# LayerNorm of the conv head: statistics spread through DRAM and applied in the channel layout, in place of a second set of transposes

## The chip, the cores and the metric

The kernel runs on one core of a Trainium2 chip. The metric is the device time of one execution in microseconds (us). Shown with the kernel before are three timed runs, and one further execution that the hardware profiler recorded instruction by instruction; durations and waits below are from that one. The engines are named as in the profile: PE (TensorE matmul) and PEld (its weight load), DVE (VectorE), ACT (ScalarE), POOL (GpSimd), SP (SyncE, whose queue issues every DMA of this kernel).

## The reference

One layer of a hybrid encoder in fp32 over two sequences (256 and 2048 tokens, with 16 meta tokens prepended). RMSNorm, one input projection of 1024 to 2816 columns, a windowed attention group, a convolution group, gates, one output projection, residual. The part around the change is the convolution group:

```python
def conformer_conv(c_val, c_glu, conv_w, conv_b, ln_w, ln_b):
    u = c_val * jax.nn.sigmoid(c_glu)
    y = depthwise_conv(u, conv_w, width=31) + conv_b        # over time, per channel
    return jax.nn.silu(layernorm(y, ln_w, ln_b))            # over the 512 channels of a token

cnv   = conformer_conv(...) * jax.nn.silu(g_conv)
mixed = jnp.concatenate([att, cnv], axis=-1)
out   = z + jnp.einsum('ble,ed->bld', mixed, w_out)
```

So each token needs a mean and a variance over its 512 channels, and is then scaled, shifted (per channel) and passed through SiLU.

## The kernel before

**Tiling.** Tokens go in 18 blocks of 128 (two of the prompt, sixteen of the sample) and six groups of three blocks. The input projection is cut into eleven units of 256 columns. It runs in two halves, c = 0 (groups 0 to 2) and c = 1 (groups 3 to 5); in each half the units come in the order: four conv units, two conv gates, two attention gates, one k/v unit, two q units. Every projection is a PSUM tile `pj` of 24 matmuls (eight pieces of the inner dimension, three passes each with the high and low parts of a split fp32), and projections are numbered pj1, pj2 and so on. Through most of the first stage a projection takes PSUM banks tagged "a" and "b" in turn, two of each, so projection n takes the bank of projection n-4.

**The q units.** A projection of a q unit (24 matmuls of 256 columns) is squared and summed on ACT (`ssq`), POOL makes the reciprocal root (`rqq`, lines 148 and 149), and DVE multiplies PSUM by it (`qs`, line 1010). Only then is the bank free. In c = 0 the second q unit is pj68 to pj76, block 0 to 8; pj77 is the first projection of c = 1, and from there a projection has 384 columns.

**The conv group.** The product u of value and gate lies with channels on partitions (four tiles of 128 channels, j = 0 to 3) and time along the free axis. The 31 taps of the convolution run on DVE into `y`, which again has channels on partitions.

**LayerNorm, one block at a time** (`ln_block`, line 211 on). Stage s1: four PE transposes (`lnt`, line 221) bring 128 tokens by 512 channels into a PSUM bank of tag "c", tokens on partitions. DVE takes bn_stats and bn_aggr, and POOL makes the reciprocal deviation r and -mean*r (`mv`, three small operations, lines 148, 149, 227). Stage s2: one DVE tensor_scalar from PSUM makes the normalised block `zn`, a scalar pair per partition (line 234). Stage s3: four PE transposes back (`lnu`, line 240), then four ACT SiLU (line 243) with the channels' weight and bias as per-partition scale and bias. Then `zn` is stored to a DRAM buffer `cd`. The blocks of c = 0 are done while the q units of c = 0 and the first conv units of c = 1 run; those of c = 1 during the q units of c = 1.

**What sets the order.** A clock of ticks runs through the program, about one per projection; `later(k, f)` puts a step k ticks on, and `owe` and a credit pace the conv taps among the projections. A scheduler then orders each engine's instructions at build time, by its own estimate of times; on the chip each engine runs its list in order and waits on semaphores. From the call of `attention_open` on (in the q units of c = 1), POOL keeps the program's order. In the second stage each block's attention and its output projection (`y`, line 609) alternate on PE. It reads the normalised conv blocks back from `cd` (`cn`), multiplies them on POOL by the gate `gc`, and splits the product into high and low parts (`mch`, `mcl`). The tiles `gc`, `cn`, `ga` and others of that stage take the memory of the LayerNorm tiles (`mixing_open` closes one pool and opens the other).

SP issues its DMAs in order, and each waits until the one eight before it has landed, since eight semaphores are used in turn.

Of the kernel before, what the change touches and what calls it, by code (L numbers as in the profile page):

```python
# [11 lines left out]
F32 = mybir.dt.float32  # L12
# [35 lines left out]
W0 = 3  # L48
LN_WAIT = (9, 1)
LTAGS = "dbdbd" + "dcdcddddd"  # L50
LTAGS_N = len(LTAGS)
# [48 lines left out]
def hymba_kernel(  # L100
# [24 lines left out]
    cd = dram.tile([NB, P, 512], F32, name="cd")  # L125
    wod = dram.tile([8, 2, P, D], F32, name="wod")

    ident = const.tile([P, P], F32, name="ident")
# [78 lines left out]
    cp = right_pools.enter_context(tc.tile_pool(name="cp", bufs=4, side="right"))  # L207
    yt = {}
    phase = [1]

    def ln_block(c, b, ready):
# [6 lines left out]
        def s1():  # L218
            pt = psum.tile([P, 512], F32, tag="c", name=f"lnt{b}")
            for j in range(NJ):  # L220
                nc.tensor.transpose(pt[:, P * j : P * j + P], yt[c, j][:, o : o + P], ident)
            bs = yp.tile([P, 6], F32, tag="bs", name=f"bs{b}")
            mv = yp.tile([P, 3], F32, tag="mv", name=f"mv{b}")
            nc.vector.bn_stats(out=bs, in_=pt)
            nc.vector.bn_aggr(out=mv[:, 0:2], in_=bs)
            rsqrt(mv[:, 1:2], mv[:, 1:2], 1.0, LN_EPS)
            nc.gpsimd.tensor_scalar(mv[:, 2:3], mv[:, 0:1], mv[:, 1:2], -1.0, op0=ALU.mult, op1=ALU.mult)
            st["pt"], st["mv"] = pt, mv
            later(1, s2)

        def s2():
            st["zn"] = yp.tile([P, 512], F32, tag="zn", name=f"zn{b}", bufs=3)
            mv = st["mv"]
            nc.vector.tensor_scalar(st["zn"], st["pt"], mv[:, 1:2], mv[:, 2:3], op0=ALU.mult, op1=ALU.add)
            later(1, s3)

        def s3():
            pt = psum.tile([P, 512], F32, tag="d" if phase[0] == 1 else "a", name=f"lnu{b}")
            for j in range(NJ):
                nc.tensor.transpose(pt[:, P * j : P * j + P], st["zn"][:, P * j : P * j + P], ident)  # L240
            cn = st["zn"].rearrange("p (j n) -> p j n", n=P)
            for j in range(NJ):
                nc.scalar.activation(
                    cn[:, j, :], pt[:, P * j : P * j + P], AF.Silu, bias=lb[:, j : j + 1], scale=lw[:, j : j + 1]
                )
            later(1, lambda: nc.sync.dma_start(cd[b], st["zn"]))

# [32 lines left out]
    def mixing_open():  # L280

        while ln_q:
            tick(0)
        flush(max(0, 4 - clock[0] + ln_at[0]))
        y_pools.close()
# [415 lines left out]
    if True:  # L701
        rows0 = {}
        sq0 = yp.tile([P, YW], F32, tag="y", name="sq0")

# [4 lines left out]
        def stats(i):  # L709
# [5 lines left out]
            elif i == 4:  # L715
                xn = yp.tile([P, YW], F32, tag="y", name=f"xn{i}")[:, :D]
            else:
# [90 lines left out]
        def weights(k):  # L808
# [4 lines left out]
            def load(eng):  # L813
# [8 lines left out]
                for q in range(4):  # L822
                    if k == 1:
                        if q % 2 == 0:
                            pair = yp.tile([P, YW], F32, tag="y", name=f"wraw{k}_{q}")
                        raw[q] = pair[:, 512 * (q % 2) : 512 * (q % 2) + 512].rearrange("p (a n) -> p a n", n=UW)
# [97 lines left out]
        def conv(c, j, part):  # L924
# [4 lines left out]
            def alloc():  # L929
                yt[c, j] = yp.tile([P, YW], F32, tag="y", name=f"y{c}_{j}")  # L930
                if c == 1:
                    nc.scalar.copy(yt[c, j][:, 0:YC], ycarry[:, j, :])

            def tap(k):
                y, u = yt[c, j], us[c, j]
                if k == 0:
# [86 lines left out]
        def kv_block(ws, g, o, rows, b):  # L1023
# [8 lines left out]
            kn = sp.tile([P, KV, 2, HD], F32, tag="kn", name=f"kn{b}")  # L1032
            owe(800)

# [285 lines left out]
```

## Time and profile before

| | |
|---|---|
| median of 3 runs | 948.61 us (948.51 to 950.12) |
| the profiled execution | 947.32 us |
| its span, first to last instruction | 945.3 us |
| granted TensorE clock | 1.000 |
| PE busy | 938.1 us (99% of the span) |
| DVE, ACT, POOL busy | 748.8, 424.1, 296.7 us |
| DMA moved | 176.49 MB, mean 187 GB/s |

A group row of the profile reads: line, engine, operation, output tile <- input tiles, shapes, count, then busy time and mean duration in ns of one, then the idle time of its engine just before it with what ended it. A row for a stretch gives each engine's busy time with its count of instructions in brackets. PE's matmuls overlap: a record of 270 ns can be followed by the next after 109 ns, so the cost of a matmul on PE is read from the distance of starts.

### The profile page before, as it was taken

To read this page: it belongs to the slowest core of one execution; us is meant where nothing else is said; L and a number is where in the kernel's file an instruction comes from. 1 tells how busy PE (TensorE), PEld (TensorE's weight loads), DVE (VectorE), ACT (ScalarE), POOL (GpSimd) and SP (SyncE) were. 2 spreads that over 40 slices of the span, in tenths; PEclk is the share of its full clock that TensorE was granted. 3 is DMA by queue.
4 is the path that set the end of the run, shared out by engine and by line. 5 is a ranking of instruction groups with operands and counts; after the bars stand their busy time and mean duration, and the time that the engine had idled before them with its cause. 6 is when DMAs were issued, how large, how long until landed. Compare 5 with 4: busy or idle time off the path is not lost.

```text
span 945.3 us, 16681 instructions
## 1 busy us (share of the span) xinstructions
PE 938.1 (99%) x5813; PEld 887.7 (94%) x5813; DVE 748.8 (79%) x1263; ACT 424.1 (45%) x1160; POOL 296.7 (31%) x490
## 2 busy tenths in 40 slices
PE   8999999999999999999999999999999999999998
PEld 8999999999999999999999999988888888888887
DVE  5579999997987879999995655687777677767763
ACT  7432022253457751011111456566666566656661
POOL 4310000183478400000000453755433243333332
PEclk9999999999999999999999999999999999999999
DMA  8585345686556595223333496985666556655512
GB/s 305 169 275 193 134 176 176 222 277 236 159 187 190 187 328 175 89 111 135 140 130 123 138 353 189 398 260 156 197 188 174 152 162 192 187 164 143 165 64 67
DMA packets 148659, 176.49 MB, mean 187 GB/s; under 512 B 40704, under 2 KB 111184, under 8 KB 148448
## 3 DMA queue, kind: packets, MB, share of 16 engines
q1 hardware_dynamic: 148576, 175.43, 57.4%
q8 instruction: 46, 0.75, 0.3%
q14 instruction: 37, 0.30, 0.1%
HBM read 112.69 MB, written 62.70 MB: 186 GB/s over the span
## 4 chain that ended last, share of the span: by engine, by line
PE 85%; DMA 5%; DVE 4%; SPq 2%; POOL 1%; ACT 1%; issue 1%; DVEq 0%; POOLq 0%; ACTq 0%
PE pj L863 41%; PE y L609 21%; PE pj L879 8%; PE O L533 5%; PE S L383 4%; PE pT_c L499 2%; PE pT_m L499 2%; PE pT_x L499 1%; DMA kw<-kd 1%; DMA qd<-qr 1%; DVE xt L772 1%; DVE y L946 1%; PE qT L383 1%; DMA cd<-zn 1%; DMA wraw<-in_w_in 1%
## 5 line engine op out<-in xcount | busy, mean ns | idle before, releaser
L863 PE MATMUL pj<-xh,ws 128*128 128x384 f32 (+1 forms) x1536 | 395.9, 338 | 0.1
L946 DVE SCALAR_TENSOR_TENSOR y<-us,cw,y 128x1167 f32<-128x1167 f32 x240 | 329.0, 1428 | 0.4
L863 PEld LDWEIGHTS pj<-xh,ws 128*128 128x128 f32 x1536 | 280.0, 188 | 0.4 <-ACT xh L1116 0.4
L863 PE MATMUL pj<-xl,ws 128*128 128x384 f32 (+1 forms) x768 | 260.8, 340 | 0.1
L609 PE MATMUL y<-wo,rest 128*128 128x512 f32 (+1 forms) x672 | 173.2, 395 | 0.0
L879 PE MATMUL pj<-ws,xh 128*128 128x256 f32 (+1 forms) x880 | 165.8, 284 | 0.9 <-ACT sqq L980 0.5
L863 PEld LDWEIGHTS pj<-xl,ws 128*128 128x128 f32 x768 | 144.1, 188 | 0.5 <-DVE xl L801 0.4
L879 PEld LDWEIGHTS pj<-ws,xh 128*128 128x128 f32 (+1 forms) x880 | 136.5, 187 | 2.3 <-ACT sqq L980 0.8
L609 PEld LDWEIGHTS y<-wo,rest 128*128 128x128 f32 x672 | 117.5, 189 | 21.7 <-DVE rest L566 0.3
L879 PE MATMUL pj<-ws,xl 128*128 128x256 f32 (+1 forms) x440 | 124.3, 283 | 0.0
L441 DVE CUSTOM_DVE_ANT_0 sb<-S,bias,vec 128x304 f32<-128x304 f32 (+5 forms) x144 | 74.4, 517 | 32.2 <-PE S L383 31.4
L453 ACT ACTIVATE sb<-sb,nm 128x304 f32<-128x304 f32 (+5 forms) x144 | 77.8, 541 | 48.9 <-DVE nm L441 48.2
L971 ACT ACTIVATE go<-pj 128x384 f32<-128x384 f32 x48 | 23.5, 490 | 149.8 <-PE pj L863 138.3
L879 PEld LDWEIGHTS pj<-ws,xl 128*128 128x128 f32 (+1 forms) x440 | 82.2, 187 | 0.2
L561 POOL TENSOR_TENSOR at<-at,ga 128x256 f32<-128x256 f32 x36 | 26.5, 735 | 164.8 <-DVE at L555 105.1
L479 POOL TENSOR_SCALAR sb<-sb,es 128x304 f32<-128x304 f32 (+5 forms) x144 | 73.1, 526 | 16.0 <-DVE es L466 13.2
L148 POOL TENSOR_SCALAR ssk<-ssk 128x2 f32<-128x2 f32 x18 | 7.5, 419 | 213.1 <-ACT sqk L985 211.1
L383 PEld LDWEIGHTS S<-kw,q 128*128 128x128 f32 x288 | 53.2, 188 | 11.3 <-issue 0.3
L383 PE MATMUL S<-kw,q 128*128 128x304 f32 (+5 forms) x288 | 62.7, 299 | 0.2 <-issue 0.2
L148 POOL TENSOR_SCALAR ssq<-ssq 128x4 f32<-128x4 f32 (+2 forms) x55 | 26.4, 479 | 96.5 <-ACT xn L726 73.6
L906 ACT ACTIVATE sg<-pj 128x384 f32<-128x384 f32 (+1 forms) x24 | 11.8, 492 | 83.1 <-PE pj L863 66.1
L609 PE MATMUL y<-wo,mch 128*128 128x512 f32 x144 | 47.2, 409 | 0.0
(139 smaller groups left out, 1317.7 us busy)
## 6 DMA issues: line engine op xcount, KB each, us to landing
wd<-ws SPq DMA_DIRECT2D x36, 512.0 KB, 6.0
ws<-wd SPq DMA_DIRECT2D x36, 512.0 KB, 6.0
wraw<-in_w_in SPq DMA_DIRECT2D x52, 256.0 KB, 6.4
xn<-in_z SPq DMA_DIRECT2D x18, 512.0 KB, 5.5
gd<-go SPq DMA_DIRECT2D x48, 192.0 KB, 2.1
yo<-in_z SPq DMA_DIRECT2D x36, 256.0 KB, 3.9
out_y<-yo SPq DMA_DIRECT2D x35, 256.0 KB, 2.6
wo<-wod SPq DMA_DIRECT2D x16, 512.0 KB, 7.5
```

What stands on the lines that cost most here:

```text
L148: nc.gpsimd.tensor_scalar(src, src, scale, eps, op0=ALU.mult, op1=ALU.add)
L383: r = f(*a, **k)
L441: nc.vector.tensor_tensor_reduce(out=sb[:, n, c0:c1], in0=ps[:, 0:w], in1=cst["bias"][:, kv, at + c0 : at + c1], scale=1.0, scalar=nsnk[:, ...
L453: nc.scalar.activation(sb[:, n, c0:c1], sb[:, n, c0:c1], AF.Exp, bias=nm[:, n : n + 1], scale=-1.0, accum_out=rs[:, n : n + 1],)
L479: nc.gpsimd.tensor_scalar(sb[:, k, a0:a1], sb[:, k, a0:a1], es[:, k : k + 1], 1.0, op0=ALU.mult, op1=ALU.mult)
L499: nc.tensor.transpose(pt[: c1 - c0, n, :], sbt[b, kv][:, n, c0:c1], ident)
L533: nc.tensor.matmul(opj[b, kv][:, n0:n1], t[:r, kv, :], p[:r, n0:n1], start=(k == "c" and i == 0), stop=(k == "x" and i == len(work) - 1),)
L561: nc.gpsimd.tensor_tensor(at[:, pr, :], at[:, pr, :], gat[b][:, pr, :], op=ALU.mult)
L609: nc.tensor.matmul(ps, mh[mi][:, e % 4, :], wo[e, wi][:, cols], start=(e == 4 and k == 0), stop=(e == 3 and k == 2),)
L863: nc.tensor.matmul(ps[:, :n], ws[:, d, wi, P * half_i : P * half_i + P], x[xi][:, d, o : o + n], start=(k == 0), stop=(k == 3 * ND - 1),)
L879: nc.tensor.matmul(ps[:rows, :UW], x[xi][:, d, o : o + rows], ws[:, d, wi, :], start=(k == 0), stop=(k == 3 * ND - 1),)
L946: nc.vector.scalar_tensor_tensor(y[:, yo + o0 : yo + o1], u[:, o0 + k : o1 + k], cw[:, j, k : k + 1], y[:, yo + o0 : yo + o1], op0=ALU.mul ...
```

## The change

The transposes back are dropped. After s1, the two numbers per token (r and -mean*r, 128 x 2 values) are stored to a small DRAM buffer `sd` two ticks later. At the third tick they are loaded into every partition (`lnb`, a broadcast load of 256 values to 128 partitions). Two ticks after that, DVE multiplies the four channel tiles of `y` by r and POOL adds -mean*r, both as 128 x 512 tensor_tensor over SBUF operands. One tick later, ACT applies the four SiLU, now from SBUF, and the block is stored to `cd` as before. The four `y` tiles become one tile `ybig`, so that one instruction can span them; the borrowed uses of that memory at the start follow. The number of ticks run when the second stage opens follows the longer chain. For blocks 8 to 17 the k/v unit holds back the conv taps by a credit of 200 instead of 800.

```diff
+LN_STEPS = (2, 3, 2)
+    sd = dram.tile([NB, P, 2], F32, name="sd")
-    yt = {}
+    ybig = yp.tile([P, NJ, YW], F32, tag="y", name="ybig", bufs=1)
+    normed = [0]
         def s1():
             pt = psum.tile([P, 512], F32, tag="c", name=f"lnt{b}")
             for j in range(NJ):
-                nc.tensor.transpose(pt[:, P * j : P * j + P], yt[c, j][:, o : o + P], ident)
+                nc.tensor.transpose(pt[:, P * j : P * j + P], ybig[:, j, o : o + P], ident)
...
-            st["pt"], st["mv"] = pt, mv
-            later(1, s2)
+            later(LN_STEPS[0], lambda: nc.sync.dma_start(sd[b], mv[:, 1:3]))
+            later(LN_STEPS[1], s2)
 
         def s2():
-            st["zn"] = yp.tile([P, 512], F32, tag="zn", name=f"zn{b}", bufs=3)
-            mv = st["mv"]
-            nc.vector.tensor_scalar(st["zn"], st["pt"], mv[:, 1:2], mv[:, 2:3], op0=ALU.mult, op1=ALU.add)
-            later(1, s3)
+            st["bc"] = yp.tile([P, P, 2], F32, tag="bc", name=f"lnb{b}", bufs=3)
+            nc.sync.dma_start(st["bc"].rearrange("p n a -> p (n a)"), sd[b : b + 1].rearrange("a n c -> a (n c)").to_broadcast([P, 2 * P]))
+            later(LN_STEPS[2], s3)
+
+        def spread(k):
+            return st["bc"][:, :, k].unsqueeze(1).to_broadcast([P, NJ, P])
 
         def s3():
-            pt = psum.tile([P, 512], F32, tag="d" if phase[0] == 1 else "a", name=f"lnu{b}")
+            st["zn"] = yp.tile([P, NJ, P], F32, tag="zn", name=f"zn{b}", bufs=3)
+            nc.vector.tensor_tensor(st["zn"], ybig[:, :, o : o + P], spread(0), op=ALU.mult)
+            nc.gpsimd.tensor_tensor(st["zn"], st["zn"], spread(1), op=ALU.add)
+            normed[0] += 1
+            later(1, s4)
+
+        def s4():
+            zn = st["zn"]
             for j in range(NJ):
-                nc.tensor.transpose(pt[:, P * j : P * j + P], st["zn"][:, P * j : P * j + P], ident)
...
+                nc.scalar.activation(zn[:, j, :], zn[:, j, :], AF.Silu, bias=lb[:, j : j + 1], scale=lw[:, j : j + 1])
+            later(1, lambda: nc.sync.dma_start(cd[b], zn.rearrange("p j n -> p (j n)")))
...
-        flush(max(0, 4 - clock[0] + ln_at[0]))
+        flush(max(0, sum(LN_STEPS[1:]) + 3 - clock[0] + ln_at[0]))
...
-            owe(800)
+            owe(800 if b < 8 else 200)
```

The scheduler's order around the LayerNorm blocks changes with it. At three places the orders are shown.

POOL, at the second q unit of c = 0, before, up to the reciprocal root of block 5 (`xl` is the low part of the next group's input, of which POOL makes half; the number behind `ssq_` and `rqq_` is the block):

```order
L149 TENSOR_TENSOR rqq_4_3155<-ssq_4_3149,half 128x4
L801 TENSOR_TENSOR xl_3263<-xt_0_2932,xh_3262 128x384
L148 TENSOR_SCALAR ssq_5_3224<-ssq_5_3224 128x4
L801 TENSOR_TENSOR xl_3263<-xt_1_2934,xh_3262 128x384
L149 TENSOR_TENSOR rqq_5_3230<-ssq_5_3224,half 128x4
```

The same place with the change:

```order
L245 TENSOR_TENSOR zn_3294<-zn_3294,lnb_3169 128x512
L150 TENSOR_SCALAR mv_3161<-mv_3161 128x1
L808 TENSOR_TENSOR xl_3245<-xt_1_2928,xh_3244 128x384
L808 TENSOR_TENSOR xl_3245<-xt_2_2930,xh_3244 128x384
L808 TENSOR_TENSOR xl_3245<-xt_3_2932,xh_3244 128x384
L150 TENSOR_SCALAR ssq_5_3212<-ssq_5_3212 128x4
L151 TENSOR_TENSOR mv_3161<-mv_3161,half 128x1
L150 TENSOR_SCALAR mv_3227<-mv_3227 128x1
L150 TENSOR_SCALAR mv_3286<-mv_3286 128x1
L150 TENSOR_SCALAR ssq_6_3271<-ssq_6_3271 128x4
L245 TENSOR_TENSOR zn_3369<-zn_3369,lnb_3235 128x512
L151 TENSOR_TENSOR rqq_5_3218<-ssq_5_3212,half 128x4
```

Two subtractions stood between the reciprocal roots of blocks 4 and 5. There now stand two adds of the LayerNorm, statistics of further blocks and all four subtractions of that group (the first of them one row above the excerpt, block 4's root three rows above it).

PE, where c = 1 begins, with the change (pj79 and pj80 belong to group 4, pj81 to group 5):

```order
L870 MATMUL pj79_3572<-xh4_3244,ws1_0_2874 128x384
L870 MATMUL pj81_3654<-xh5_3462,ws1_0_2874 128x384
L870 MATMUL pj81_3654<-xl5_3463,ws1_0_2874 128x384
L870 MATMUL pj81_3654<-xh5_3462,ws1_0_2874 128x384 x2
L870 MATMUL pj81_3654<-xl5_3463,ws1_0_2874 128x384
L870 MATMUL pj80_3609<-xh4_3244,ws1_0_2874 128x384
```

Before, pj80 followed pj79 directly; now five matmuls of pj81 stand ahead of it, and no `lnu` stands anywhere.

SP, where the second stage's first loads stand, before:

```order
L195 DMA qd<-qr_16_6066 128x256
L368 DMA gc_6253<-gd 128x4x128
L195 DMA qd<-qr_17_6139 128x256
L370 DMA cn_6255<-cd 128x512
L364 DMA ga_6299<-gd 128x4x128
L368 DMA gc_6614<-gd 128x4x128
L360 DMA wo_6320<-wod 128x1024 x3
L360 DMA wo_6365<-wod 128x1024 x3
```

With the change, the last of the block stores and loads ahead of `gc` and `cn`:

```order
L253 DMA cd<-zn_6068 128x512
L197 DMA qd<-qr_9_6164 128x256
L197 DMA qd<-qr_10_6217 128x256
L367 DMA wo_6550<-wod 128x1024
L367 DMA wo_6499<-wod 128x1024
L197 DMA qd<-qr_11_6263 128x256
L367 DMA wo_6499<-wod 128x1024 x2
L367 DMA wo_6550<-wod 128x1024
L197 DMA qd<-qr_12_6320 128x256
L367 DMA wo_6550<-wod 128x1024
L375 DMA gc_6225<-gd 128x4x128
L377 DMA cn_6227<-cd 128x512
```

Six more loads of `wo` stand further up, so the first `gc` and `cn` come behind twelve of them, where before they came ahead of all.

More of the change, by code (lines that the diff above doesn't have):

```diff
@@ L702, in hymba_kernel @@
         rows0 = {}
-        sq0 = yp.tile([P, YW], F32, tag="y", name="sq0")
+        sq0 = ybig[:, 0]
         def pinned(op, yes=True):
@@ L715, in stats @@
             elif i == 4:
-                xn = yp.tile([P, YW], F32, tag="y", name=f"xn{i}")[:, :D]
+                xn = ybig[:, 1, :D]
             else:
@@ L824, in load @@
                         if q % 2 == 0:
-                            pair = yp.tile([P, YW], F32, tag="y", name=f"wraw{k}_{q}")
+                            pair = ybig[:, 2 + q // 2]
                         raw[q] = pair[:, 512 * (q % 2) : 512 * (q % 2) + 512].rearrange("p (a n) -> p a n", n=UW)
@@ L929, in alloc @@
             def alloc():
-                yt[c, j] = yp.tile([P, YW], F32, tag="y", name=f"y{c}_{j}")
                 if c == 1:
-                    nc.scalar.copy(yt[c, j][:, 0:YC], ycarry[:, j, :])
+                    assert normed[0] == 8
+                    nc.scalar.copy(ybig[:, j, 0:YC], ycarry[:, j, :])
             def tap(k):
-                y, u = yt[c, j], us[c, j]
+                y, u = ybig[:, j], us[c, j]
                 if k == 0:
```

6 lines of the change are left out of this document (removed).

## Prediction

> **What bounds the kernel now.** I read the page first: the busy shares, then the chain of waits.
>
> ```profile
> span 945.3 us, 16681 instructions
> PE 938.1 (99%) x5813; PEld 887.7 (94%) x5813; DVE 748.8 (79%) x1263; ACT 424.1 (45%) x1160; POOL 296.7 (31%) x490
> PE 85%; DMA 5%; DVE 4%; SPq 2%; POOL 1%; ACT 1%; issue 1%; DVEq 0%; POOLq 0%; ACTq 0%
> ```
>
> PE is busy in 99% of the span and holds 85% of the chain. An instruction taken off PE shortens the end by its slot, unless what replaces it makes PE wait. POOL's 31% is an average, so I then read the stretches in which LayerNorm blocks run (columns: PE, PEld, DVE, ACT, POOL, clock, DMA share, GB/s).
>
> ```profile
> 285.00:305.00 20.00, 19.85 (x169) 19.61 (x169) 15.91 (x31) 15.91 (x72) 17.69 (x25) 1.00 0.60 179
> 305.00:325.00 20.00, 20.00 (x126) 19.94 (x125) 16.07 (x32) 16.84 (x38) 11.32 (x21) 1.00 0.52 166
> 585.00:600.00 15.00, 15.00 (x127) 14.87 (x126) 9.78 (x33) 10.03 (x33) 8.11 (x17) 1.00 1.01 353
> 600.00:615.00 15.00, 14.48 (x101) 13.17 (x101) 8.94 (x29) 9.48 (x29) 10.92 (x23) 1.00 1.05 396
> ```
>
> PE has no hole worth naming at 285 to 325 us, but POOL is busy for 17.69 of 20 us there: that is where the change adds work to POOL. At 585 to 615 us, where the second stage opens, the DMA engines are full.
>
> **Removed from PE.** The record of one transpose says 270 ns; its slot is the distance of starts.
>
> ```profile
> L240 PE MATMUL lnu<-ident,zn x72: 270/272/273, 293.9 to 577.5; 128*128 128x128 f32 x72
> 548.35 0.60 PE L240 MATMUL lnu<-ident,zn 128*128 128x128 f32 x4
> 548.78 0.49 PE L221 MATMUL lnt<-ident,y 128*128 128x128 f32 x3
> ```
>
> Four take 548.78 - 548.35 = 0.43 us, 0.108 each. 72 of them: -7.8 us. The orders agree that exactly these 72 leave PE and nothing joins it.
>
> **Changed on the other engines.** First the durations of what goes and of the nearest likes of what comes.
>
> ```profile
> L234 DVE TENSOR_SCALAR zn<-lnt,mv x18: 798/810/814, 291.6 to 575.4; 128x512 f32<-128x512 f32 x18
> L579 POOL TENSOR_TENSOR cn<-cn,gc x18: 1277/1286/1473, 603.2 to 914.1; 128x512 f32<-128x512 f32 x18
> L586 ACT CAST mch<-cn x9: 605/621/626, 607.1 to 896.0; 128x512 fp32r<-128x512 f32 x9
> L587 DVE TENSOR_TENSOR mcl<-cn,mch x9: 682/693/695, 607.9 to 896.6; 128x512 fp32r<-128x512 f32 x9
> ```
>
> DVE gives a 0.81 us pass from PSUM for one of about 0.69 from SBUF: 18 times, a small gain, hidden under PE. ACT keeps its 72 SiLU, with another source; ACT was busy for 15.91 of 20 us at most, so I count nothing. POOL gets 18 adds of 1.286 us, 23.1 us in all, eight of them in c = 0 (10.3 us) in a stretch where it had 2.3 us of 20 free. SP gets 36 DMAs; their nearest likes:
>
> ```profile
> vc<-vd SPq DMA_DIRECT2D x18, 128.0 KB, 3.8
> vm<-vmd SPq DMA_DIRECT2D x8, 16.0 KB, 2.1
> ```
>
> Store and load back take some 2.1 + 3.8 = 5.9 us, against ticks of about one projection, 2.8 us in this stretch (seven up to the start of pj77, quoted below). The load stands one tick behind the store, the product two behind the load. That is covered by other work, except where the queue is full (below).
>
> **What POOL's adds hold up.** DVE frees the bank of a q projection only after POOL's reciprocal root. I add up POOL's list between the roots of blocks 1 and 5 of the second q unit (rqq1, rqq5), with the means of this stretch (285.3 to 310.7 us):
>
> ```profile
> L149 POOL TENSOR_TENSOR rqq<-ssq,half 128x4 f32<-128x4 f32 x8 | 8.4, 1054 | 0.3
> L801 POOL TENSOR_TENSOR xl<-xt,xh 128x384 fp32r<-128x384 f32 x8 | 8.4, 1049 | 1.6 <-ACT xh L791 1.3
> L149 POOL TENSOR_TENSOR mv<-mv,half 128x1 f32<-128x1 f32 x4 | 2.9, 729 | 0.1
> L148 POOL TENSOR_SCALAR ssq<-ssq 128x4 f32<-128x4 f32 x7 | 2.1, 307 | 0.6
> L227 POOL TENSOR_SCALAR mv<-mv 128x1 f32<-128x1 f32 x4 | 1.0, 261 | 0.1
> L148 POOL TENSOR_SCALAR mv<-mv 128x1 f32<-128x1 f32 x4 | 1.0, 239 | 0.3
> ```
>
> Before: 6 xl, 4 ssq, 4 rqq and two of each mv step, 6.29 + 1.23 + 4.22 + 2.46 = 14.2 us, and 1.3 idle for xh. The rows below give the start and the check: rqq1 ends at 284.31 + 1.01 = 285.3, so rqq5 should end at 300.8, and it ends at 299.88 + 1.02 = 300.9.
>
> ```profile
> 284.31 1.01 POOL L149 TENSOR_TENSOR rqq<-ssq,half 128x4 f32<-128x4 f32 x1
> 299.88 1.02 POOL L149 TENSOR_TENSOR rqq<-ssq,half 128x4 f32<-128x4 f32 x1
> 304.87 0.34 PE L863 MATMUL pj<-xh,ws 128*128 128x384 f32 x1
> 285.35 0.42 DVE L1010 TENSOR_TENSOR qs<-pj,rqq 128x256 f32<-128x256 f32 x1 [1.31 <-PE pj L879]
> 49.57 169.23 PE pj L863 x957
> ```
>
> pj77, which needs that bank, starts at 304.87: 3.5 us to spare after the 0.42 of qs. With the change the list to rqq5 is 8 xl, 3 adds, 5 ssq, 4 rqq and 6 + 4 + 3 mv steps: 8.39 + 3.86 + 1.54 + 4.22 + 1.43 + 2.92 + 0.78 = 23.1 us, no idle time counted. It ends at 308.4, qs at 308.9. PE comes to pj77 at 304.87 + 1.2 (two sets of `lnt` and three small transposes that stand ahead of it now) = 306.1, so it waits 2.8 us. On to rqq8 the list holds 12 xl, 6 adds, 7 ssq, 7 rqq and eight of each mv step in all: 12.59 + 7.72 + 2.15 + 7.38 + 9.83 = 39.7 us, qs at 325.4. Its bank is pj80's. Three projections of 24 x 169.23/957 = 4.24 us and the five matmuls of pj81 bring PE there at 308.9 + 13.6 = 322.5, and it waits another 2.9: 5.7 us in all. 5.7 is the sum by means; the mv steps also ran faster:
>
> ```profile
> L148 POOL TENSOR_SCALAR mv<-mv x18: 190/191/383, 287.8 to 572.1; 128x1 f32<-128x1 f32 x18
> L149 POOL TENSOR_TENSOR mv<-mv,half x18: 539/550/866, 289.4 to 572.3; 128x1 f32<-128x1 f32 x18
> ```
>
> With 0.55 for the mv roots and 0.19 for the other small steps ahead of a root, the two sums are 21.5 and 37.0, the waits 1.1 and 2.0, 3.1 us in all. The bound below is 0, if roots are made earlier than the list's sum says (no stall can gain). I take +3.5: near the sum by medians, since the means hold operations that a neighbour disturbed.
>
> **Opening of the second stage.**
>
> ```profile
> 584.71 0.42 SPq L370 DMA_DIRECT2D cn<-cd  x1
> 586.33 4.10 SPq L360 DMA_DIRECT2D wo<-wod  x6
> ```
>
> ```profile
> wo<-wod SPq DMA_DIRECT2D x16, 512.0 KB, 7.5
> 604.76 0.39 PE L879 MATMUL pj<-ws,xh 128*128 128x256 f32 x1 [0.52 <-ACT sqq L980]
> 608.88 0.48 PE L609 MATMUL y<-wo,mch 128*128 128x512 f32 x1
> DMA to landing us min/median/max: 2.8/4.0/8.9
> ```
>
> (The last row is of `cn`.) `gc` and `cn` now stand behind twelve `wo` loads, 6.3 MB, 15.9 us at the 396 GB/s of 600 to 615. With all of it some 4 us earlier: 582.3 + 15.9 + 4.0 + the gate product 1.29, cast 0.62, subtraction 0.69 = 604.8, against a first output projection at about 604.9. Just in time, and three whole projections (8.5 us) stand right ahead of it as cover. Bounds: -0.5 (the wait at 604.76 goes) to +4.9 (landing in 8.9 instead of 4.0); I take +0.7, near the median. The smaller credit lets the conv taps of c = 1 end earlier. Their last one, and the first transposes that need them, before:
>
> ```profile
> L946 DVE SCALAR_TENSOR_TENSOR y<-us,cw,y x240: 1414/1427/1440, 61.6 to 524.9; 128x1167 f32<-128x1167 f32 x120
> 533.42 0.60 PE L221 MATMUL lnt<-ident,y 128*128 128x128 f32 x4
> ```
>
> The taps end at 524.9 + 1.4 = 526.3, 7 us ahead of the transposes, which now stand one projection (2.8 us) earlier: 4 us stay, so I count nothing for it.
>
> **Sum.** -7.8 + 3.5 + 0.7 = -3.6. The profiled execution took 947.32, so 943.7; the median of the runs lies 1.3 above it: **945.0 us**.
>
> **Rivals.**
>
> *The full gain.* POOL's list is made shorter by starting the statistics earlier, and a bank in hand covers the rest. For: PE's order puts only five matmuls of another projection ahead of pj80. Against: the sums above. -7.8: 939.5, median 940.8.
>
> *The pair DVE and POOL stand in each other's way, and the gain is used up.* One small operation on POOL, twice:
>
> ```profile
> 260.96 1.31 POOL L148 TENSOR_SCALAR ssq<-ssq 128x4 f32<-128x4 f32 x1 [0.83 <-DVE ssq L981]
> 284.04 0.19 POOL L148 TENSOR_SCALAR ssq<-ssq 128x4 f32<-128x4 f32 x1 [0.45 <-ACT sqq L985]
> ```
>
> 1.31 while DVE runs conv taps, 0.19 alone. DVE's pass came from PSUM; now product and add both read SBUF. If each of the six adds ahead of rqq8 waits out one DVE pass of 0.69, that is 4.1 us more: -7.8 + 3.5 + 4.1 + 0.7 = +0.5, 947.8, median 949.1: no change. Against: DVE is 80% busy here, much of it from PSUM. The Trainium skill, "SBUF — State Buffer", section "Who interferes with whom", says that a VectorE instruction with two SBUF inputs and a GpSimd one that reads SBUF exclude each other for a whole instruction, while one with a single SBUF input does not; by that rule the change makes a conflict where there was none, and the two rows agree with such a lock.
>
> *Slower: the second stage opens late.* The round trip of the last blocks falls where DMA is full. If store and load take their longest instead of their median, 8.0 for 2.4 and 8.9 for 4.0 (rows of `zn` here, of `cn` above), the last block, and with it the memory that `gc` and `cn` take over, is 10.5 us late.
>
> ```profile
> DMA to landing us min/median/max: 2.0/2.4/8.0
> ```
>
> It decides from 4.3 us on (7.8 - 3.5). -7.8 + 3.5 + 10.5 = +6.2: 953.5, median 954.8. Against: medians held in the same stretch before.
>
> **Chances.** Forecast 0.43, full gain 0.25, DVE against POOL 0.20, late opening 0.12. A measurement tells about 0.2% (1.9 us) from no change, so faster is below 946.7 and slower above 950.5. Faster: 0.37 of the forecast, all of the full gain, 0.03 of the third: 0.65. Same: 0.06 + 0.14 + 0.01 = 0.21. Slower: 0.14. The range runs from 940.2 to 950.5; the forecast alone from 943.4 (waits 3.1, opening -0.5) to 947.2 (waits 5.7).
>
> **What would show it.** 72 fewer PE matmuls. PE waits on DVE `qs` between about 306 and 325 us, of 2 to 6 us together, with POOL nearly full; none there means the full gain. `zn` adds well over 1.3 us, or small POOL steps near 1.3, mean the third case. A first output projection later than about 606 us, with waits for `cn` or `ga`, means the fourth. I am wrong altogether if the time is lost elsewhere: conv taps of c = 1 starting late, or SP held by a store's landing.

## The result: slower by 5.9%, and the profile after

The changed kernel took **1005.2 us** (median of four runs, 1003.4 to 1006.7), the kernel before beside it 948.8. The ratio is 1.059, 95% interval 1.057 to 1.061: 56.4 us lost where a gain of 3.6 was forecast. The page of the changed kernel (busy time of the engines, granted clock in 40 slices, chain of waits):

```profile
span 1003.8 us, 16624 instructions
PE 952.9 (95%) x5741; PEld 898.4 (90%) x5741; DVE 754.6 (75%) x1263; ACT 434.3 (43%) x1166; POOL 323.9 (32%) x508
PEclk9999999999998899999999997899999999999999
PE 78%; DMA 10%; ACT 4%; issue 3%; DVE 2%; POOL 2%; SPq 1%; DVEq 0%; POOLq 0%; ACTq 0%
```

The 72 transposes are gone (5813 - 5741 matmul records), yet PE's busy time grew from 938.1 to 952.9 us and its share fell to 95%. DMA holds 10% of the chain for 5% before. The clock row has an 8 or a 7 at two places, about 300 to 350 us and 600 to 650 us; before it was 9 throughout. Span less busy time is PE's idle time: 50.9 us for 7.2 before. The stretches that the prediction read, now (same columns):

```profile
285.00:305.00 20.00, 14.06 (x98) 13.49 (x96) 9.87 (x19) 10.84 (x49) 14.38 (x22) 0.83 0.59 113
305.00:325.00 20.00, 14.06 (x94) 13.40 (x95) 15.39 (x32) 11.19 (x43) 12.74 (x20) 0.88 0.62 155
585.00:600.00 15.00, 12.03 (x91) 11.82 (x90) 6.93 (x25) 4.64 (x13) 7.89 (x18) 0.89 0.67 101
600.00:615.00 15.00, 9.81 (x70) 9.64 (x70) 4.58 (x13) 7.30 (x18) 5.80 (x10) 0.84 0.93 283
```

PE had no hole at 285 to 325 us; it now idles 6 of every 20 us. POOL, which was to be the full engine, is *less* busy in the first of these stretches (14.38 for 17.69 us), although it has the adds on top: it waits too. The first output projection tells where the time is gone:

```profile
L616 PE MATMUL y<-wo,mch x144: 387/393/496, 665.9 to 979.6; 128*128 128x512 f32 x144
```

It starts at 665.9 us for 608.9, that is 57 us later. From there to the end it is 338 us, before 336. So the whole loss lies in the two stretches with LayerNorm blocks, and none in the second stage proper.

Who waits there: DVE's waits, then those of SP's queue (engine, line, for whom: us in all, times, longest).

```profile
DVE zn L244 <- DMA lnb<-sd: 47.6, 10, 8.4
DVE zn L244 <- DMA cd<-zn: 8.2, 1, 8.2
```

```profile
SPq L236 <- DMA sd<-mv: 42.1, 13, 7.4
```

DVE stands 47.6 us for the load `lnb`, and SP stands 42.1 us for the store `sd` before it can issue that load. One trip on DVE and on SP (start, duration, instruction, idle time before it):

```profile
287.69 1.81 DVE L808 TENSOR_TENSOR xl<-xt,xh 128x384 fp32r<-128x384 f32 x2
296.29 0.69 DVE L244 TENSOR_TENSOR zn<-ybig,lnb 128x512 f32<-128x512 f32 x1 [6.79 <-DMA lnb<-sd]
296.90 0.69 DVE L227 BATCH_NORM_STATS2 bs<-lnt 128x6 f32<-128x512 f32 x1
```

```profile
293.03 1.02 SPq L231 DMA_DIRECT2D sd<-mv  x1
298.85 0.37 SPq L750 DMA_DIRECT2D xt<-in_zt  x1
302.27 0.34 SPq L236 DMA_DIRECT2D lnb<-sd  x1
303.02 0.34 SPq L253 DMA_DIRECT2D cd<-zn  x1
```

DVE does nothing for 6.79 us, because the product stands ahead of the next statistics in its list; those read the PSUM bank that the next `lnt` on PE needs. On SP, the load that waits for the store of 293.03 follows only at 302.27, 9.2 us behind it, for 1 KB. The list of DMAs (KB each, median us from issue to landing) says that such landings are common:

```profile
cd<-zn SPq DMA_DIRECT2D x18, 256.0 KB, 5.4
lnb<-sd SPq DMA_DIRECT2D x18, 128.0 KB, 5.0
sd<-mv SPq DMA_DIRECT2D x18, 1.0 KB, 7.3
```

The prediction had 2.1 us for this store and 3.8 for the load. Its 2.1 us come from `vm<-vmd`, which is not a store but a load of 16 KB, in rows of 1 KB. And a third party is hit: the stores to `cd`, as large as ever, land after 5.4 us for 2.4.

### The profile page after: what moved, and what is told of

Read it like the earlier page. It is cut to its first block, busy times and chain, and to the rows that moved or that the text cites. A ratio compares the mean times of both kernels' runs of the same rounds, so it can differ in the third digit from the quotient of the medians.

```text
span 1003.8 us, 16624 instructions
## 1 busy us (share of the span) xinstructions
PE 952.9 (95%) x5741; PEld 898.4 (90%) x5741; DVE 754.6 (75%) x1263; ACT 434.3 (43%) x1166; POOL 323.9 (32%) x508
## 4 chain that ended last, share of the span: by engine, by line
PE 78%; DMA 10%; ACT 4%; issue 3%; DVE 2%; POOL 2%; SPq 1%; DVEq 0%; POOLq 0%; ACTq 0%
PE pj L870 40%; PE y L616 20%; PE pj L886 5%; PE O L540 5%; PE S L390 4%; DMA sd<-mv 3%; DMA lnb<-sd 2%; PE pT_m L506 1%; PE pT_c L506 1%; PE pT_x L506 1%; DMA bias<-in_bias_c 1%; DMA ws<-wd 1%; DMA cn<-cd 1%; DMA cd<-zn 1%; DVE ybig L953 1%
## 5 line engine op out<-in xcount | busy, mean ns | idle before, releaser
L953 DVE SCALAR_TENSOR_TENSOR ybig<-us,cw,ybig 128x1167 f32<-128x1167 f32 x240 | 329.1, 1433 | 0.3
L870 PEld LDWEIGHTS pj<-xh,ws 128*128 128x128 f32 x1536 | 282.9, 190 | 9.1 <-DVE us L925 4.6
L886 PE MATMUL pj<-ws,xh 128*128 128x256 f32 (+1 forms) x880 | 174.4, 294 | 1.0 <-DVE kn L1044 1.0
L886 PEld LDWEIGHTS pj<-ws,xh 128*128 128x128 f32 (+1 forms) x880 | 144.4, 197 | 1.9 <-ACT sqq L987 1.2
L616 PEld LDWEIGHTS y<-wo,rest 128*128 128x128 f32 x672 | 117.5, 189 | 21.7 <-DVE rest L573 0.3
L886 PE MATMUL pj<-ws,xl 128*128 128x256 f32 (+1 forms) x440 | 128.2, 291 | 0.0
L460 ACT ACTIVATE sb<-sb,nm 128x304 f32<-128x304 f32 (+5 forms) x144 | 77.8, 540 | 56.6 <-DVE nm L448 55.6
L886 PEld LDWEIGHTS pj<-ws,xl 128*128 128x128 f32 (+1 forms) x440 | 86.6, 197 | 0.3
L390 PE MATMUL S<-kw,q 128*128 128x304 f32 (+5 forms) x288 | 64.9, 309 | 16.1 <-DVE nm L448 8.8
L244 DVE TENSOR_TENSOR zn<-ybig,lnb 128x512 f32<-128x512 f32 x18 | 14.6, 813 | 55.7 <-DMA lnb<-sd 47.6
```

Source lines behind the costliest of these rows:

```text
L390: r = f(*a, **k)
L460: nc.scalar.activation(sb[:, n, c0:c1], sb[:, n, c0:c1], AF.Exp, bias=nm[:, n : n + 1], scale=-1.0, accum_out=rs[:, n : n + 1],)
L616: nc.tensor.matmul(ps, mh[mi][:, e % 4, :], wo[e, wi][:, cols], start=(e == 4 and k == 0), stop=(e == 3 and k == 2),)
L870: nc.tensor.matmul(ps[:, :n], ws[:, d, wi, P * half_i : P * half_i + P], x[xi][:, d, o : o + n], start=(k == 0), stop=(k == 3 * ND - 1),)
L886: nc.tensor.matmul(ps[:rows, :UW], x[xi][:, d, o : o + rows], ws[:, d, wi, :], start=(k == 0), stop=(k == 3 * ND - 1),)
L953: nc.vector.scalar_tensor_tensor(y[:, yo + o0 : yo + o1], u[:, o0 + k : o1 + k], cw[:, j, k : k + 1], y[:, yo + o0 : yo + o1], op0=ALU.mul ...
```

## The experiments

Times are medians beside the kernel before on the same chip (947.3 to 949.0 us). Line numbers in rows are those of each kernel. In what was expected, T is the theory of the trip (its landings are late and lists stand behind them) and P that of POOL (its adds); R and Q are explained in each place. e1, e2, e5 and e6 leave the normalisation's two numbers out of what they compute (a constant stands for them).

### Off the whole change: trip, distance, queue, buffers

**e1_no_trip**: neither store nor load; product and add read one constant tile.

```diff
-            later(LN_STEPS[0], lambda: nc.sync.dma_start(sd[b], mv[:, 1:3]))
-            st["bc"] = yp.tile(...); nc.sync.dma_start(st["bc"]..., sd[b]... to all partitions)
+            st["bc"] = bcc        # memset to 0.5 once
```

> The change without its round trip: no store of the two numbers and no load back; product and add read one constant tile, filled once at the start (so the normalisation is left out of the output). All PE, DVE, POOL and ACT instructions stay. Theory T (the round trip through DRAM comes later than the order built for it allows; DVE stands in its list at the product, PE stands behind DVE and its clock falls to half): the 47.6 us of DVE waits on the load go, PE's waits with them, and the time is 938 to 946 us, clock 1.0. Rival P (POOL's adds keep banks of the q projections, as forecast): PE still waits 2 to 6 us in all around 306 to 325 us, 943 to 947. If it is neither (the merged tile, the smaller credit), the time stays above 990.

971.0 us, 1.024 (1.022 to 1.026). The trip is worth 34 us, but 23 of loss stay, which neither theory had.

**e2_no_dep**: store and load both, the load from a buffer that 18 stores at the start filled, so that it waits for nothing.

> Both transfers stay, but the load reads another DRAM buffer that is filled once at the start, so it does not wait for the store (the normalisation is left out of the output). T with the store's landing as its larger half (median 7.3 us against 5.0 of the load, and SP stands still meanwhile): 955 to 985 us, DVE waits on the load about halved. If only the load's own landing counted: near 1005.

1009.9 us (one run), near the second number, but not for its reason. At the start, where the 18 further stores stand, PE has a wait of 12.5 us that the change doesn't have; without it some 997 us would be left. DVE has no wait for `lnb` at all any more, but a longer one for the landings of `cd` (8.2 us in the change):

```profile
DVE zn L249 <- DMA cd<-zn: 27.2, 8, 9.0
```

So with both transfers still there, taking the wait for the load away brings little.

**e3_long** (`LN_STEPS = (2, 5, 5)`, `LN_WAIT = (4, 1)`: three ticks more between load and product, two more ahead of the load, the blocks of c = 0 five ticks earlier) and **e4_act_queue** (store and load issued by ACT in place of SP):

> The change with more ticks in the chain: load five ticks behind the statistics instead of three, product five ticks behind the load instead of two; the blocks of c = 0 start five ticks earlier to make room. T (lateness against the order): DVE's waits on the load fall to under 15 us and the time to 945 to 970 us. If the 36 transfers or their issue on SP cost by themselves: no better than 995.

> The change with the store and the load back issued on ACT's queue instead of SP's. Rival Q (the two small transfers queue behind SP's bulk loads): their landings fall from 7.3 and 5.0 us to 2 to 3.5 us, SP no longer stands still, and the time is 945 to 975 us. If small transfers are slow by themselves: landings as before, 995 to 1020, with ACT standing where SP stood.

1007.3 and 996.2 us (one run each). Longer steps halved DVE's wait for the load (47.6 us before) and brought no time:

```profile
DVE zn L244 <- DMA lnb<-sd: 24.2, 5, 7.5
```

The sum of such waits is therefore not what the trip costs. On ACT's queue the landings came after 5.9 and 4.4 us for 7.3 and 5.0, far from the 2 to 3.5 of rival Q, and the wait for the store's landing holds ACT instead of SP: 23 us in nine waits, on four kinds of ACT instructions.

**e11_rings**: more buffers for all that the trip holds (`mv` 8, `lnb` 5, `zn` 6).

> The changed kernel (1005 us) with more buffers for what the trip holds: eight of mv, five of lnb, six of zn for four, three and three. Theory T: nothing of note changes, 995 to 1010 us. Theory R (a block can't start because the buffers of an earlier one are held until its transfers have landed): 975 us or less.

1001.5 us, 1.056 (1.053 to 1.058). Theory T's number; buffers are not the cause.

### The 23 us that stay without the trip: POOL's add

**e5_no_add** is e1 without `nc.gpsimd.tensor_tensor(... op=ALU.add)`; **e6_ring** is e1 with six buffers of `zn`.

> As e1_no_trip (no store, no load, the product reads a constant tile), and POOL's 18 adds are left out too, so that ACT's SiLU reads what DVE's product wrote; the normalisation is not computed. e1_no_trip had holes of 23.6 us in PE's matmuls at 275 to 360 us and of 12.4 us at 545 to 675 us. Theory P (POOL: its adds of 1.3 us each, and what stands ahead of them in its list, hold zn and with it DVE and PE): both holes go, and the full gain of the 72 transposes comes: 938 to 945 us. Theory R (three buffers of zn, each held until its store to cd has landed, with DVE's product ahead of the statistics in DVE's list): the wait of the product for cd stays, 955 to 970 us.

> As e1_no_trip, with six buffers of zn for three; the normalisation is not computed. Theory R: the product no longer waits for cd (12.6 us in six waits in e1_no_trip), the holes go, 938 to 947 us. Theory P: the adds are as late as before and little changes, 962 to 972 us.

957.6 us, 1.010 (1.008 to 1.011), and 971.6 us, 1.024 (1.023 to 1.026). They differ by 14 us for the adds, and e6 doesn't differ from e1, so the ring of `zn` is not the cause. The adds are a part only: e5 came out at theory R's number, not at P's, and is still 16 us behind a full gain. A reason for these 16 us is at hand but was only argued. With no trip to wait for, the build puts the products far ahead in DVE's list (the first at 279 us, before its own block's statistics at 287), where they wait for something else:

```profile
291.87 1.31 DVE L244 TENSOR_TENSOR zn<-ybig,bcc 128x512 f32<-128x512 f32 x2 [4.09 <-DMA cd<-zn]
```

(e1, DVE in order of time.) Taking a dependency away changes every list, so from here on the edits keep the dependencies (all but e14), though the build still gives most of the kernels lists of their own.

**e7_pe_bcast** brings the two numbers to all partitions by PE: two transposes of a column of `mv`, spread over 128 columns, into the bank that `lnu` had. Product and add both run on DVE, from there.

```diff
-LN_STEPS = (2, 3, 2)
+LN_STEPS = (1, 1, 1)
...
-            st["bc"] = yp.tile(...); nc.sync.dma_start(...)
+            st["bc"] = psum.tile([P, 512], F32, tag="d" if phase[0] == 1 else "a", name=f"lnb{b}")
+            for k in range(2):
+                nc.tensor.transpose(st["bc"][:, P*k : P*k + P], st["mv"][:, k+1 : k+2].to_broadcast([P, P]), ident)
-            nc.gpsimd.tensor_tensor(st["zn"], st["zn"], spread(1), op=ALU.add)
+            nc.vector.tensor_tensor(st["zn"], st["zn"], spread(1), op=ALU.add)
```

> The whole LayerNorm, with the two numbers brought to all partitions by two transposes on PE into a PSUM bank in place of the trip through DRAM, and product and add both on DVE, from there. 36 transposes fewer than before on PE, 36 x 0.108 = 3.9 us. If the trip and POOL's adds (theories T and P) are what costs: 942 to 946 us, no holes. If it is that the channels' layout keeps ybig and zn longer, or DVE's 18 further passes of some 0.8 us (14.6 us) in its in-order list: 952 us or more, with holes at 285 to 350 us.

**944.3 us**, 0.995 (0.993 to 0.997): faster than both kernels, by 4.8 us where 3.9 was worked out. It keeps the merged tile `ybig` and the smaller credit of the change, so these two cost nothing of note. **e10_pool_add** is the same with the add back on POOL (ACT copies -mean*r from PSUM to SBUF for it).

> As e7_pe_bcast (944.3 us; numbers brought by PE), with the add back on POOL as in the change: ACT copies the second number from PSUM to SBUF, POOL adds from there, 18 adds of 1.286 us. It prices the prediction's term for POOL alone: +3.1 to +5.7 us by that term, 947 to 950 us, with PE waiting for DVE's qs at 305 to 325 us. If POOL's adds are worth what e5_no_add took off e1_no_trip (13 us): 955 us or more. If they cost nothing: 944 to 945 us.

956.5 us, 1.008 (1.006 to 1.010). The two differ by 12.7 us, each taken against its own kernel before. ACT's copy is in these 12.7 (POOL stands still for it for 20.7 us in eleven waits); e5 and e6, which have no copy, had put the adds at 14. e7's stretches, then e10's (columns as above), and e10's longest wait of PE:

```profile
285.00:305.00 20.00, 19.27 (x165) 19.03 (x165) 17.31 (x33) 15.28 (x68) 18.66 (x29) 1.00 0.57 172
305.00:325.00 20.00, 20.00 (x131) 19.81 (x129) 19.31 (x39) 16.48 (x47) 14.05 (x25) 1.00 0.59 187
```

```profile
285.00:305.00 20.00, 18.11 (x142) 17.73 (x141) 16.89 (x34) 15.09 (x64) 18.91 (x27) 0.91 0.47 147
305.00:325.00 20.00, 16.43 (x104) 15.96 (x103) 17.53 (x27) 13.73 (x45) 18.91 (x27) 0.91 0.48 152
```

```profile
PE pj L872 <- DVE qs L1019: 2.3, 1, 2.3
```

With the adds POOL is busy 18.91 of 20 us in both stretches, and PE idles for 1.9 and 3.6 us, with the clock at 0.91. The wait for `qs`, 2.3 us, is the one that the prediction priced; it is a small part of the 12.7.

### On the kernel before: the trip alone

Here the kernel before keeps its own LayerNorm, and the trip is added beside it.

**e8_before_trip** adds store, load, and a copy of two columns on DVE (0.17 us) that waits for the load; **e9_no_reader** is the same without the copy; **e13_store_only** has only the store.

```diff
+            later(2, lambda: nc.sync.dma_start(sd[b], mv[:, 1:3]))       # e8, e9, e13
+            later(3, t2)                                                 # e8, e9
+        def t2():
+            bc = yp.tile([P, P, 2], F32, tag="bc", name=f"lnb{b}", bufs=3)
+            nc.sync.dma_start(bc.rearrange("p n a -> p (n a)"), sd[b : b + 1].rearrange("a n c -> a (n c)").to_broadcast([P, 2 * P]))
+            later(2, lambda: nc.vector.tensor_copy(jk, bc[:, 0, :]))     # e8
```

> The kernel before, unchanged in what it computes, plus the store of 1 KB and the load to all partitions of each block at the ticks the change uses, and a copy of two columns on DVE that waits for the load; nothing else needs it. Theory T (a DRAM trip costs because an instruction in DVE's in-order list waits for its landing, and what is behind it on DVE and PE waits too): 965 us or more, waits of DVE for lnb as long as in the changed kernel (47.6 us in ten). If the trip costs only by what it makes late (zn, the stores to cd, the opening of the second stage): 947 to 953 us.

> As e8_before_trip (986.5 us), with store and load but without the small copy on DVE: nobody waits for the load. Theory T (DVE held by a landing): the 36 transfers alone cost next to nothing, 947 to 952 us. Theory Q (the transfers themselves, SP held by a store's landing while other issues stand behind the load in its list): 965 us or more, with waits of DVE for xt and of others for loads that SP issues late.

> As e9_no_reader (975.3 us) without the load: 18 stores of 1 KB and nothing that waits for them. Theory Q1 (SP's list stands still while the load waits for the store): 947 to 951 us. Theory Q2 (the transfers themselves): between, 955 to 970 us.

986.5 us (1.040, 1.038 to 1.041), 975.3 us (1.028, 1.026 to 1.030) and 964.0 us (1.016, 1.013 to 1.019). So the copy costs 10.7 us, the load 11.3, and the bare store 15.3, although nobody waits for what it brings. Theory T explains only the first. That first price is the cleanest: apart from the copy and one matmul's place, all engines run the same lists in e8 and e9. e8 on DVE, in order of time, and e9's waits of SP:

```profile
301.09 0.17 DVE L238 COPY jk<-lnb 128x2 f32<-128x2 f32 x1 [6.33 <-DMA lnb<-sd]
```

```profile
SPq L236 <- DMA sd<-mv: 30.8, 12, 5.1
```

An instruction of 0.17 us stops DVE for 6.33, and PE then stands for 5.9 us, up to 303.84, for a `qs` of DVE. In e9 it is SP's list that stands; how much of the 11.3 us is that and how much the load's own transfer, no run tells apart (e14 was to).

**e12_far_reader** puts e8's copy eight ticks behind the load for two; **e15_late_load** puts e9's load at ten ticks for three.

> As e8_before_trip, with the small copy on DVE eight ticks behind the load for two (and buffers enough for it). Theory T with the distance as the mis-sized thing (two ticks are too few where a landing takes 3 to 9 us and SP issues late): the copy finds its data there, 948 to 956 us. If the wait follows the instruction wherever it stands, because the build puts it where it thinks that the load has landed: 970 us or more.

> As e9_no_reader, with the load at ten ticks behind the statistics for three, that is eight behind the store for one. If the distance is what was mis-sized: SP's waits for sd go and the time is 947 to 955 us. If the build's list keeps the load close behind the store all the same, the waits stay: 965 us or more.

984.8 us (1.038, 1.036 to 1.041) and 975.7 us (1.028, 1.025 to 1.032): both times as if nothing had been done. In e12 nothing was: all engines run the lists of e8, with the copy in the same place, 3.2 to 8.7 us behind the load's issue (e8: 3.3 to 8.5). The ticks only say in which order the program names its steps; the build then puts an instruction where by its estimate the data is there, and that estimate is short of the landings. What a copy that really stands further behind would cost, e12 doesn't say. In e15 the later loads did move back, and SP's waits for `sd` fell to 23.9 us from 30.8, without a gain. e12's waits:

```profile
DVE jk L238 <- DMA lnb<-sd: 37.8, 15, 6.2
```

**e14_const_load** (both transfers; the load reads a constant):

> As e9_no_reader, with the load reading a constant that was stored once at the start, so that it doesn't wait for the block's store; both transfers stay. Theory Q1: 947 to 953 us, no wait of SP for sd. Theory Q2: 965 us or more.

982.2 us (1.035, 1.032 to 1.037), and no answer to its question. With nothing to wait for, the 18 loads were built in at 17 to 51 us, where PE then waited 14.7 us for POOL's roots; theory Q2's number came for another reason. One thing can be read from it: with no load in the later list PE has, as in e13, no hole of note at 275 to 360 us (busy 83.7 and 84.0 of 85 us), so e9's loss there (77.8) belongs to the load.

### Why a store of 1 KB costs 15 us

The stretches where e13 loses its time, before and in e13:

```profile
545.00:555.00 10.00, 10.00 (x88) 10.00 (x87) 6.97 (x24) 5.41 (x15) 5.40 (x16) 1.00 1.04 350
555.00:560.00 5.00, 5.00 (x45) 5.00 (x45) 2.25 (x5) 1.78 (x5) 2.80 (x7) 1.00 0.99 374
```

```profile
545.00:555.00 10.00, 9.03 (x78) 8.85 (x77) 4.88 (x11) 5.41 (x15) 3.81 (x9) 1.00 0.75 279
555.00:560.00 5.00, 2.75 (x24) 2.55 (x22) 0.54 (x5) 0.48 (x2) 1.72 (x7) 1.00 1.26 167
570.00:580.00 10.00, 6.72 (x58) 6.52 (x57) 2.63 (x7) 3.10 (x9) 3.23 (x8) 0.95 0.90 268
```

The last two columns are the DMA engines' share and the GB/s. At 555 to 560 us the engines are full in both, but move 167 GB/s for 374. What is different is the store: 128 pieces of 8 bytes. The chain from there to PE, on DVE and then PE in e13:

```profile
579.69 0.81 DVE L240 TENSOR_SCALAR zn<-lnt,mv 128x512 f32<-128x512 f32 x1 [6.25 <-DMA cd<-zn]
```

```profile
580.55 1.11 PE L246 MATMUL lnu<-ident,zn 128*128 128x128 f32 x4 [3.83 <-DVE zn L240]
```

The stores to `cd` land late, so none of the three buffers of `zn` is free, DVE's pass waits, and PE waits for it. DVE's waits for `cd` as a whole, before and in e13:

```profile
DVE zn L234 <- DMA cd<-zn: 5.8, 3, 3.4
```

```profile
DVE zn L240 <- DMA cd<-zn: 24.8, 5, 6.2
```

**e16_big_pieces** and **e17_small_pieces** test this. Both add to e13 one small POOL operation that spreads a number of `mv` over a row of two partitions. e16 stores that row (two pieces of 512 bytes, 1 KB), e17 stores `mv` as e13 does (128 pieces of 8 bytes, 1 KB). The lists of PE and POOL are the same in both; DVE's and ACT's differ in one instruction's place each, SP's in some ten places, mostly by a place or two.

> The kernel before plus one store of 1 KB per block, as two pieces of 512 bytes (a row of numbers that a small POOL operation spreads over two partitions behind the statistics). Nobody waits for it. Cause 1 (pieces of 8 bytes): 948 to 951 us, stores to cd landing after 2.4 us again. Cause 2 (a further store in SP's list): 960 to 966 us, as e13_store_only.

> The same as e16_big_pieces with the same small POOL operation, but the store is the one of e13_store_only, 128 pieces of 8 bytes. By both causes 960 to 966 us; it is what e16_big_pieces is compared with.

**952.5 us** (1.005, 1.003 to 1.006) and **970.7 us** (1.024, 1.022 to 1.026): 18.2 us for the pieces. With the same bytes, their size, their number and the partitions that they are read from go together; the runs don't part these. e17 is above the 960 to 966 us that both causes gave; it has the POOL operation besides e13's store. At 560 to 570 us, e16 and then e17:

```profile
560.00:570.00 10.00, 10.00 (x88) 10.00 (x87) 5.24 (x13) 4.84 (x14) 4.03 (x13) 1.00 1.04 381
```

```profile
560.00:570.00 10.00, 6.66 (x44) 6.48 (x43) 3.73 (x16) 1.78 (x5) 3.61 (x12) 0.83 0.85 145
```

The same two in the count of packets and in DVE's waits for `cd`:

```profile
DMA packets 148732, 176.51 MB, mean 186 GB/s; under 512 B 40740, under 2 KB 111256, under 8 KB 148520
DVE zn L242 <- DMA cd<-zn: 3.4, 2, 2.3
```

```profile
DMA packets 151252, 176.52 MB, mean 182 GB/s; under 512 B 43296, under 2 KB 113776, under 8 KB 151040
DVE zn L242 <- DMA cd<-zn: 17.3, 4, 5.6
```

2520 packets more of 151252, with the same bytes, bring DVE's waits for `cd` from 3.4 to 17.3 us. (Landings can't be compared: e16's trace gives them for two of its 18 stores to `cd` alone.) The small pieces take next to nothing themselves: in the DMA records from 545 to 600 us one of 8 bytes takes 9 ns in e17, while a packet of 2 KB takes 125 ns in the mean for 93 in e16. The Trainium skill, "DMA: Bandwidth & Descriptors", section "Specifications", puts the least transfer for full rate at 512 B and says that below it the DMA engine reads, modifies and writes. The two runs agree as to the side of 512 B; that such pieces also slow the large transfers beside them is what they add. e16 is not free either: 5.1 us stay for the POOL operation and a further store, more than cause 1 allowed; the two are not told apart.

**e18_row_trip** puts this into the change: one PE transpose per block turns r and -mean*r into two rows, ACT copies them out of PSUM, and the store has two pieces of 512 bytes.

> The whole change, with the two numbers per token turned into two rows by one PE transpose per block (18 x 0.108 = 1.9 us) and copied by ACT, so that the store has two pieces of 512 bytes. If the pieces of 8 bytes are a part of the change's loss, 980 to 992 us (1005.2 less 15 to 25); what then stays is the waiting for the two landings in the lists of SP and DVE, and POOL's adds. If they are not, 1003 to 1010 us.

**979.6 us**, 1.034 (1.032 to 1.036): 24 us better than the change, with one transpose per block more. (In `lnb` the two numbers now lie in rows instead of in pairs; the medians of product and add hardly change by it, 692 for 692 and 1291 for 1298 ns.) SP's and DVE's waits for the trip fall with it, from 42.1 and 47.6 us:

```profile
SPq L243 <- DMA sd<-rw: 9.2, 7, 3.2
```

```profile
DVE zn L251 <- DMA lnb<-sd: 14.7, 9, 5.8
```

### The account

| part of the change | us | from |
|---|---|---|
| 72 transposes leave PE | -7.8 | the prediction; e7 bears it out for 36 (-3.9 worked out, -4.8 measured) |
| POOL's 18 adds (with ACT's copy) | +12.7 | e10 less e7 |
| the store | +15.3 | e13 |
| the load: its transfer, and SP's list standing for the store | +11.3 | e9 less e13 |
| one DVE instruction that waits for the load | +10.7 | e8 less e9 |
| sum | +42.2 | |
| measured | +56.4 | |

The 14 us between have no run of their own. In the change a large pass waits with more behind it, not a copy of 0.17 us, and the pieces alone are worth 24 there (e18) for 15 beside the kernel before; but a sum of parts taken from several kernels with several orders need not close.

Read downwards from the change, each run against its own kernel before, the same loss goes like this: the store in two pieces takes 24.1 us off it (e18), no trip at all 9.0 more (e1), no adds 14.7 more (e5). What is left is 8.6 us above the kernel before, where 7.8 below it was due: 16.4 us that no run names, in kernels whose lists the build made anew.

## Why the prediction was wrong, step by step

- **"Removed from PE": right.** Exactly 72 matmuls fewer, and e7 shows that such a saving does arrive when nothing waits.
- **"Store and load back take some 2.1 + 3.8 = 5.9 us ... covered by ticks of 2.8 us": this is the step that failed.** It was put at nothing and cost most of the loss: 37.4 us beside the kernel before (e8), 34 in the change (1005.2 less e1's 971.0). It failed in three ways. The price: the store was taken from a load of 16 KB that lands in 2.1 us, and took 7.3. Bytes were compared, where the pieces count (e16, e17). The cover: ticks were read as time, and e12 shows that six ticks more can leave an instruction where it was, e15 and e3 that even later steps gain nothing. And the side effects were left out: the store slows `cd` (15.3 us with no reader at all, e13), SP stands behind the store, and the product stands in DVE's list ahead of statistics that PE waits for. The prediction named who waits at the q units, and not what is queued behind the product and the load.
- **"What POOL's adds hold up": right in place and direction, a third of the size.** +3.5 was taken (3.1 to 5.7), 12.7 was measured. POOL is full as the sum said (18.91 of 20 us), and PE waits for `qs` at 313 to 315 us in e10, for 2.3 us. The waits at `lnt` (1.9 us), at e10's own transposes (1.3 and 1.2) and the fall of the clock were not in the sum.
- **"Opening of the second stage", +0.7, from 604.8 against 604.9 us: wrong.** The first output projection came 57 us late. The blocks themselves were late (stores to `cd` until 644 us, before 581), which the term didn't have. What the order of the DMAs added, which it did price, is not told apart: the first `cn` goes out 10.0 us behind the last of these stores, for 3.4 before, but the first output projection follows that store by 21.7 us, for 27.5 before.
- **ACT's SiLU and DVE's product at nothing: right as to their durations** (480 and 692 ns at the median), wrong as to their waits.
- **The rivals.** The full gain did not come. *DVE against POOL* is too small to be the cause: the add took 1277/1298/1665 ns (least, median, most; 1357 in the mean) for 1286 foreseen, 1.3 us over all 18, and the product 678/692/1768 (813 in the mean), 2.2 us over its median. By the Trainium skill's rule that the prediction weighed ("SBUF — State Buffer", "Who interferes with whom") the two block each other where they overlap; the few long ones agree (a product at 340.0 us took 1768 ns, the add at 339.8 took 1477), the medians show no such block in most of the 18. *The second stage opens late* had the right sign and place, with 10.5 us for 57 and a wrong reason: it let single landings be long at the end, where they were long from the first blocks on (7.3 and 5.0 us at the median over all 18). The last sentence of the prediction, "SP held by a store's landing", named a part of the cause as a thing that would make it wrong, without a price or a chance.

## What to carry to other kernels

Ask of every DRAM trip not how many bytes it has but in how many pieces it is written, what stands behind its load in the queue that issues it, and what stands behind its first reader in that engine's list; a step named later in the program is not a step later on the chip. To bring a few numbers per token to all partitions, two transposes of a spread column (0.108 us each on PE here) beat a store of 1 KB and its load to all partitions by far: with the add on POOL in both, 956.5 us (e10) against 1005.2. A prediction that lists what would make it wrong should give those things a price as well.

## What was not expected of the hardware

**Small pieces cost other transfers their rate**: 18 stores of 1 KB cost 18.2 us in pieces of 8 bytes more than in pieces of 512 (e16, e17); beside such stores the DMA engines' share stood at 1.26 while 167 GB/s were moved (e13).

**The clock falls with PE's holes.** The granted clock was 1.00 in all stretches read before. e5 has one run of holes, from 286 to 304 us:

```profile
290.00:300.00 10.00, 4.05 (x18) 2.40 (x16) 8.99 (x19) 8.76 (x35) 8.27 (x16) 0.56 0.41 106
300.00:305.00 5.00, 0.71 (x3) 0.74 (x4) 2.96 (x6) 1.16 (x5) 3.92 (x8) 0.50 0.75 270
305.00:310.00 5.00, 5.00 (x32) 5.00 (x31) 1.38 (x4) 1.76 (x11) 2.41 (x4) 0.67 0.46 158
310.00:315.00 5.00, 5.00 (x45) 5.00 (x45) 0.43 (x1) 1.85 (x12) 2.25 (x4) 1.00 0.09 30
```

In the last 5 us of the holes the clock stands at 0.50, and it is at 1.00 again from 310 us on, within 6 us of the last hole: 32 matmuls in the 5 us after it, 45 in the next. So a kernel that PE bounds pays for a hole a second time. The Trainium skill, "TensorE: Matmul & The Clock Gate", section "What's actually happening", has half rate after some 3.4 us of idling and full rate after as much of work. These rows roughly agree as to the return: PE starts again at 304.3 us (0.71 us of work up to 305), and 0.67 over the next stretch, as a mean of 0.50 and 1.00, puts full rate at an estimated 308.3, 4.0 us later. For the fall they are too coarse.
